# Moving the transposed activations by 16 bytes, and interleaving the stationary weights of two quarters of an up projection

## The chip, the cores and the metric

One core of one Trainium2 chip runs the whole program in one launch. The metric is device microseconds per execution; the time given for a kernel is the median of its runs.

## What is computed

The reference is one layer of a bidirectional encoder over 512 tokens of width 1024, in float32, with 256 memory tokens:

```python
x = x + token_mixer(rmsnorm(x, norm_mix), w_in, ...)      # HGRN2 heads and mLSTM heads, both directions
x = x + cross_attention(rmsnorm(x, norm_xattn), rmsnorm(mem, norm_mem), w_q, w_kv, w_o)
x = x + squared_relu_mlp(rmsnorm(x, norm_mlp), w_up, w_down)
return rmsnorm(x, norm_final)

def squared_relu_mlp(xn, w_up, w_down):                   # w_up: 1024 x 4096, w_down: 4096 x 1024
    return jnp.square(jax.nn.relu(xn @ w_up)) @ w_down
```

## The kernel before

**Three matmuls for one.** Every float32 operand of a projection is split into a high half, which has the type float32r, and the remainder as a low half. `mm3` (L221 to L223) multiplies high by high, high by low and low by high, and adds all three in PSUM. In the notation of the profile: L221 is stationary high and moving high, L222 stationary high and moving low, L223 stationary low and moving high.

**The weight stream.** All weights are packed by the host into 141 slices of 128 partitions by 1024 elements, in the order in which they are used (`SEQ`). `load` brings a slice into a buffer `st` by a DMA on SyncE's queue; `split` makes the halves `wh` and `wl` of it: an ACTIVATE on ScalarE (L217) writes the high half, a subtraction on VectorE (L218) the low half. There are three buffers each of `st`, `wh` and `wl`. `weights(key)` splits the slice that is needed and the two after it, and starts the load of the third after it.

**Two kinds of projection.** `proj_d` makes output with channels on partitions: the weights are stationary, 128x128 for each of eight k-tiles, and 512 tokens of activations move. A slice holds the eight k-tiles one behind the other, 128 columns (512 bytes in a partition) each: `z = slice(k * P, k * P + P)`. `proj_t` makes output with tokens on partitions: 128 tokens of activations are stationary, and 512 columns of weights move.

**Transposed activations.** The moving operand of a `proj_d` is a pair of tiles `xT` of 4096 elements, k-tiles 0 to 3 in the first, 4 to 7 in the second, each k-tile as 512 high and then 512 low elements. Three activations use the same pair in turn: the normed input (the mixer's projections), `x2T` (the query projection of the cross-attention) and `x3T` (the MLP's up projection). They are written piece by piece by L217 and L218, or by L769 and L770 in `transp`.

**The MLP.** It runs over four quarters f of the 4096 hidden channels. In each, eight slices of the up projection give eight `act` tiles (ReLU on ScalarE at L872, square on VectorE at L873, split by L217 and L218), and then `proj_t` multiplies these by eight slices of the down projection (residual add at L887). `act` lies in tiles of the tag `yT` in quarters 0 and 2, and in tiles of the tag `a4` (`a` in the profile) in quarters 1 and 3. A quarter's up and down projections have 192 matmuls of 512 columns each.

**Dependent work.** The chains of the mixer's heads advance by `tick()` between the projections. HGRN's `hgrn_chain` multiplies, level by level (L = 1, 2, 4, ... 64), a `rhs` that is gathered in place (L372), updates tiles with strided accesses (L422, L425, L429), and gathers a `kcomb` (L362):

```python
rhs=ap(q2, w * P, [2 * L, P // (2 * L)], [512 + L, 2], [1, L])     # L372
fa = ap(f, 0, [512, 2], [2 * L, nb])                               # L429, in place: fa = fa * fb
fb = ap(f, L, [512, 2], [2 * L, nb])
```

The mLSTM's chain takes two tiles of the tag `tiny2` for each of four token tiles of a head (`nd` and `rd`, L631 to L638).

**Where tiles lie.** A tag's buffers lie one behind the other, in the order in which the tags are first used, each rounded up to 32 bytes: ... `misc`, `selr`, `xT` (2 buffers of 16384 bytes), `st`, six tiny ones, `wh`, `wl` (3 of 4096 each), `a4` (10 of 4096), `t2`, `vv`, ... `yT` (8 of 4096), `tiny4`, `tiny2`. This gives the byte address in a partition: `xT` at 52512 and 68896, the first `wh` at 97760, the first `a4` at 122336, the first `yT` at 196160. [...]

The order of instructions on each engine is chosen by the tile framework's scheduler; `weights` asks for high priority.

Of the kernel before, what the change touches and what calls it, by code (L numbers as in the profile page):

```python
# [10 lines left out]
F32 = mybir.dt.float32  # L11
F32R = mybir.dt.float32r
# [6 lines left out]
P = 128  # L19
# [10 lines left out]

# columns of the per-channel vector pack
V_XATTN, V_MEM, V_MLP = 0, 8, 16
# [5 lines left out]

# columns of the constant pack
C_ID, C_MF, C_MB, C_SEL, NC1 = 0, 128, 256, 384, 392  # L40
# [35 lines left out]
def trunk(ctx: ExitStack, tc: tile.TileContext, x, mem, wpk, vec, cst, lmask, rmask, rows, out):  # L76
# [20 lines left out]
    def tiny(w):  # L97
        return sb.tile([P, w], F32, tag=f"tiny{w}", name=nm("tiny"), bufs=2 if w == 8 else 6)

    def ap(t, off, *dims):  # L100
        a = t[:, :]
        return bass.AP(a.tensor, a.offset + off, [list(a.ap[0])] + [list(d) for d in dims])
# [5 lines left out]
    VV = lambda: T("vv", 516, 8)  # L108
    XT = lambda: [T("xT", 4096, 2, F32R) for _ in range(2)]
    YT1 = lambda dt=F32R: T("yT", 1024, 8, dt)  # L110
    hl = lambda t: (t[:, 0:512], t[:, 512:1024])

# [1 line left out]
    cs = sb.tile([P, NC1], F32, name="cs")  # L114
# [50 lines left out]

# [1 line left out]
    chains = []  # L167
# [20 lines left out]

# [1 line left out]
    st_tiles, hl_tiles = {}, {}  # L190
# [8 lines left out]
    def split(i):  # L199
        if i >= len(SEQ) or i in hl_tiles:  # L200
            return
        load(i)
        s = st_tiles[i]
        hi, lo = T("wh", 1024, 3, F32R), T("wl", 1024, 3, F32R)
        split_out(hi, lo, s)
        hl_tiles[i] = (hi, lo)

    def weights(key):
# [15 lines left out]

    # activation operand accessors: list over k of (hi [P,n], lo [P,n])
    def xk(tiles, n=512):
# [7 lines left out]
    def proj_d(mat, c0, xs, n=512, count=2):  # L234
        """[128 channels, n tokens] PSUM tiles, one per slice"""
        for j in range(count):
            wh, wl = weights(("d", mat, 0, c0 + P * j))
            ps = mmb()
            for k in range(8):
                z = slice(k * P, k * P + P)  # L240
                mm3(ps[:, :n], wh[:, z], wl[:, z], xs[k][0], xs[k][1], k == 0, k == 7)
                if k == 3:
                    tick()
            yield ps
            tick()

    def proj_t(mat, k0, c0, xs, ntile=4, pre=None, late=False):
        """token-major [128 tokens, 512] PSUM tiles over 8 k-tiles (four slices)"""
        acc = [mmb() for _ in range(ntile)]

        def part(t, q, w):
            for k in range(2):
                kk = 2 * q + k
                xh, xl = xs[kk][0][:, t * P:t * P + P], xs[kk][1][:, t * P:t * P + P]
                z = slice(k * 512, k * 512 + 512)
                mm3(acc[t], xh, xl, w[0][:, z], w[1][:, z], kk == 0, kk == 7)

        for q in range(2 if late else 3):
            w = weights(("t", mat, k0 + 2 * q, c0))
            for t in range(ntile):  # L260
                part(t, q, w)
                if t % 2 == 1:
                    tick()
        if pre is not None:
            pre()
        tail = [(q, weights(("t", mat, k0 + 2 * q, c0))) for q in range(2 if late else 3, 4)]
        for t in range(ntile):
            for q, w in tail:
                part(t, q, w)
            yield t, acc[t]  # L270
            if t % 2 == 1:
                tick()

# [1 line left out]
    xT = XT()  # L275
# [25 lines left out]

# [1 line left out]
    vh = []  # L303
# [11 lines left out]

# [1 line left out]
    ys = [None] * 8  # L317
# [26 lines left out]
    def hgrn_chain(h, s_):  # L344
        q, f, k = s_["q"], s_["f"], s_["k"]
        q2 = A4()  # [b | f]
        v.tensor_tensor(out=q2[:, 0:512], in0=q[:, 0:512], in1=f[:, 512:1024], op=ALU.mult)
# [20 lines left out]
        for li, L in enumerate(LEVELS):  # L368
# [10 lines left out]
            yield  # L379
        # L = 128: adjacent windows  # L380
        ps = smb()
        for b in range(2):
            w0, w1 = slice(b * 256, b * 256 + P), slice(b * 256 + P, b * 256 + 256)
            pe.matmul(ps[:, b * 256 + P:b * 256 + 256], lhsT=k[:, w0], rhs=q2[:, 512 + b * 256 + P:512 + b * 256 + 256], start=True, stop=True)
            pe.matmul(ps[:, b * 256:b * 256 + P], lhsT=k[:, 512 + b * 256 + P:512 + b * 256 + 256], rhs=q2[:, w0], start=True, stop=True)
        # A[s-tile 2b, window 2b+1] and A[s-tile 2b+1, window 2b]
        sc.activation(ap(A, P, [1024 + 256, 2], [1, P]), ap(ps, P, [256, 2], [1, P]), AF.Copy)
        sc.activation(ap(A, 512, [1024 + 256, 2], [1, P]), ap(ps, 0, [256, 2], [1, P]), AF.Copy)
        update(q2, k, f, 128)
        yield  # L390
        # L = 256
        for dr in range(2):
# [38 lines left out]
    def head_out(o, gate, gcol, idx):  # L431
        """o [128 tokens, 4 x 128]: per-head norm, transpose, gain, gate, split into yT"""
        junk = T2()
# [17 lines left out]

# [1 line left out]
    ml = {}  # L453
# [11 lines left out]
    def gates_chain():  # L465
        grow = ml["grow"]
        ps = smb()
        for t in range(4):
            pe.transpose(ps[:, t * P:t * P + P], grow[:, t * P:t * P + P], ident)
        gt = sb.tile([P, 64], F32, name="gt")   # [w, (ig f, ig b, fg f, fg b), h]  # L470
        v.tensor_copy(gt[:, :].rearrange("p (w g h) -> p w g h", g=4, h=4), ap(ps, 0, [P, 4], [32, 4], [1, 4]))
# [17 lines left out]
        for _ in range(4):  # L489
            yield  # L490
        # token-major sums of the log forget gate
        tri = A4()
        nc.sync.dma_start(out=tri[:, 0:640], in_=cst[:, NC1:NC_])
        pb = smb()
        for i, c in enumerate((C_INC, C_SUF, C_ISUF, C_PRE, C_ONE)):
            pe.matmul(pb[:, i * 32:i * 32 + 32], lhsT=tri[:, c:c + P], rhs=lf, start=True, stop=True)
        bd = sb.tile([P, 128], F32, name="bd")  # [gap 0..3][w][dir,h]
        b4 = lambda g, w, dr: bd[:, g * 32 + w * 8 + dr * 4:g * 32 + w * 8 + dr * 4 + 4]
# [14 lines left out]
        yield  # L513
        # rows: forward heads on partitions 0..3, backward heads on 32..35
        lp = A4()
# [33 lines left out]
        for t in range(4):  # L549
            pe.transpose(ps[:, t * 64:t * 64 + 64], mr[0:64, t * P:t * P + P], ident[0:64, 0:64])  # L550
        em = sb.tile([P, 32], F32, name="em")  # [w, dir, h]
        sc.activation(em[:, :].rearrange("p (w g h) -> p w g h", g=2, h=4), ap(ps, 0, [64, 4], [32, 2], [1, 4]), AF.Exp, scale=-1.0)
# [89 lines left out]

# [1 line left out]
    hst = {}  # L644
# [52 lines left out]
    mo1 = gate_proj(4352, V_MO + 2, False)  # L697
    # memory tokens: norm and transposes
    mt = [A4(), A4()]
# [26 lines left out]

# [1 line left out]
    kT = [A4(F32R) for _ in range(4)]   # per head: [d-tile][hi 256 | lo 256]  # L728
    for i in range(4):
# [10 lines left out]

# [1 line left out]
    xr = {}  # L742
# [9 lines left out]
    def proj_res(mat, k0, src, tgt, st, pre=None):  # L752
        """residual add of a token-major projection; transposes of finished token tiles"""
        for c in range(2):
            for t, ps in proj_t(mat, k0, 512 * c, src, pre=pre if c == 0 else None):
                v.tensor_tensor(out=xr[t, c], in0=ps, in1=xr[t, c], op=ALU.add)
                stats(st, t, c)
                transp(tgt, t, c)
# [29 lines left out]

# [1 line left out]
    os_ = [None] * 8  # L790
# [61 lines left out]

# [1 line left out]
    pending = []  # L854
# [138 lines left out]
```

## Time and profile before

| | |
|---|---|
| time, median of 3 runs | 904.14 us (903.22 to 904.22) |
| span of the profiled execution | 902.4 us |
| TensorE busy (matmuls) | 884.6 us, 98% of the span |
| TensorE weight loads, beside the matmuls | 728.2 us, 81% |
| VectorE, ScalarE, GpSimd busy | 55%, 41%, 2% |
| HBM traffic | 93 GB/s over the span |

The span runs from the first to the last instruction of one profiled execution; the median of the runs lies 1.7 us above it. A matmul's row in the profile is longer than the time from one start to the next, because matmuls are pipelined: what counts below is the **pitch**, the time from one matmul's start to the next one's, which is the length of an unbroken stretch divided by its number of matmuls.

### The profile page before, as it was taken

To read this page: it belongs to the slowest core of one execution; us is meant where nothing else is said; L and a number is where in the kernel's file an instruction comes from. 1 tells how busy PE (TensorE), PEld (TensorE's weight loads), DVE (VectorE), ACT (ScalarE), POOL (GpSimd) and SP (SyncE) were. 2 spreads that over 40 slices of the span, in tenths; PEclk is the share of its full clock that TensorE was granted. 3 is DMA by queue.
4 is the path that set the end of the run, shared out by engine and by line. 5 is a ranking of instruction groups with operands and counts; after the bars stand their busy time and mean duration, and the time that the engine had idled before them with its cause. 6 is when DMAs were issued, how large, how long until landed. Compare 5 with 4: busy or idle time off the path is not lost.

```text
span 902.4 us, 11028 instructions
## 1 busy us (share of the span) xinstructions
PE 884.6 (98%) x4290; PEld 728.2 (81%) x4290; DVE 498.0 (55%) x863; ACT 371.8 (41%) x701; POOL 19.5 (2%) x49
## 2 busy tenths in 40 slices
PE   7999999999999999999999999999999999999996
PEld 5887888888876987887888888888888888888885
DVE  5457688689346977654455445433444344334443
ACT  5235443352358567454444445421332133113432
POOL 1000000010010000000000000000000000000001
PEclk9999999999999999999999999999999999999998
DMA  6321122221141232422111222222222222222212
GB/s 253 132 100 71 70 75 76 107 73 57 47 140 70 100 110 96 153 80 94 70 70 48 70 94 93 94 94 94 94 93 94 95 108 100 95 94 94 93 47 94
DMA packets 24614, 84.21 MB, mean 93 GB/s; under 512 B 2865, under 2 KB 2993, under 8 KB 24562
## 3 DMA queue, kind: packets, MB, share of 16 engines
q1 hardware_dynamic: 24272, 83.04, 25.2%
q8 instruction: 34, 0.56, 0.2%
q10 hardware_dynamic: 290, 0.47, 0.1%
q14 instruction: 18, 0.15, 0.0%
HBM read 81.40 MB, written 2.10 MB: 93 GB/s over the span
## 4 chain that ended last, share of the span: by engine, by line
PE 67%; DVE 1%; ACT 1%; issue 0%; POOL 0%; POOLq 0%; ACTq 0%
PE mm L223 20%; PE mm L222 20%; PE mm L221 20%; PE sm L625 2%; PE sm L610 2%; PE sm L764 1%; PE sm L222 1%; PE sm L221 1%; PE sm L223 1%; PE sm L821 0%; PE sm L595 0%; DVE wl L218 0%; DVE xT L770 0%; ACT wh L217 0%; POOL tiny L163 0%
## 5 line engine op out<-in xcount | busy, mean ns | idle before, releaser
L218 DVE TENSOR_TENSOR wl<-st,wh 128x1024 fp32r<-128x1024 f32 x141 | 172.7, 1224 | 272.9 <-ACT wh L217 269.5
L217 ACT ACTIVATE wh<-st 128x1024 fp32r<-128x1024 f32 x141 | 149.2, 1058 | 312.7 <-PE mm L223 167.7
L221 PE MATMUL mm<-xT,wh 128*128 128x512 f32 x552 | 221.0, 401 | 0.0
L223 PE MATMUL mm<-xT,wl 128*128 128x512 f32 x552 | 218.1, 395 | 0.0
L222 PE MATMUL mm<-xT,wh 128*128 128x512 f32 x552 | 217.6, 394 | 0.2 <-DVE xT L770 0.2
L223 PEld LDWEIGHTS mm<-xT,wl 128*128 128x128 f32 x552 | 104.1, 189 | 23.4 <-issue 0.6
L222 PEld LDWEIGHTS mm<-xT,wh 128*128 128x128 f32 x552 | 104.1, 189 | 22.6 <-DVE xT L770 0.8
L221 PEld LDWEIGHTS mm<-xT,wh 128*128 128x128 f32 x552 | 104.3, 189 | 22.4 <-issue 1.5
L223 PE MATMUL mm<-wh,yT 128*128 128x512 f32 x256 | 102.1, 399 | 0.0
L221 PE MATMUL mm<-wh,yT 128*128 128x512 f32 x256 | 102.0, 398 | 0.0
L222 PE MATMUL mm<-wl,yT 128*128 128x512 f32 x256 | 101.6, 397 | 0.0
L221 PE MATMUL mm<-wh,a 128*128 128x512 f32 x160 | 63.4, 396 | 0.0
L222 PE MATMUL mm<-wl,a 128*128 128x512 f32 x160 | 62.4, 390 | 0.0
L223 PE MATMUL mm<-wh,a 128*128 128x512 f32 x160 | 62.3, 390 | 0.0
L222 PEld LDWEIGHTS mm<-wl,yT 128*128 128x128 f32 x256 | 48.2, 188 | 11.3
L221 PEld LDWEIGHTS mm<-wh,yT 128*128 128x128 f32 x256 | 48.2, 188 | 11.3
L223 PEld LDWEIGHTS mm<-wh,yT 128*128 128x128 f32 x256 | 48.2, 188 | 11.3
L222 PEld LDWEIGHTS mm<-wl,a 128*128 128x128 f32 x160 | 30.1, 188 | 6.6 <-issue 0.5
L221 PEld LDWEIGHTS mm<-wh,a 128*128 128x128 f32 x160 | 30.0, 188 | 6.6 <-issue 0.5
L223 PEld LDWEIGHTS mm<-wh,a 128*128 128x128 f32 x160 | 30.0, 188 | 6.2
L372 PEld LDWEIGHTS sm<-a,t 128*128 128x128 f32 x224 | 30.1, 191 | 2.2 <-ACT t L362 0.4
L887 DVE SCALAR_TENSOR_TENSOR vv<-mm,misc,vv 128x512 f32<-128x512 f32 x32 | 23.3, 748 | 13.7 <-PE mm L223 13.5
(222 smaller groups left out, 1118.7 us busy)
## 6 DMA issues: line engine op xcount, KB each, us to landing
st<-in_wpk SPq DMA_DIRECT2D x141, 512.0 KB, 3.2
as<-in_x SPq DMA_DIRECT2D x4, 512.0 KB, 6.4
vv<-in_x SPq DMA_DIRECT2D x8, 256.0 KB, 4.1
out<-vv SPq DMA_DIRECT2D x7, 256.0 KB, 2.2
a<-in_mem SPq DMA_DIRECT2D x2, 512.0 KB, 3.6
t<-in_rows SPq DMA_DIRECT2D x2, 256.0 KB, 5.9
gate<-in_rows SPq DMA_DIRECT2D x1, 512.0 KB, 4.9
a<-in_lmask SPq DMA_DIRECT2D x1, 448.0 KB, 8.1
```

Source lines behind the costliest of these rows:

```text
L217: sc.activation(dst_hi, src, AF.Copy)
L218: v.tensor_tensor(out=dst_lo, in0=src, in1=dst_hi.bitcast(F32), op=ALU.subtract)
L221: pe.matmul(ps, lhsT=ah, rhs=bh, start=first, stop=False)
L222: pe.matmul(ps, lhsT=ah, rhs=bl, start=False, stop=False)
L223: pe.matmul(ps, lhsT=al, rhs=bh, start=False, stop=last)
L372: pe.matmul(ps[:, z], lhsT=kc[:, z], rhs=ap(q2, w * P, [2 * L, P // (2 * L)], [512 + L, 2], [1, L]), start=True, stop=True)
L610: pe.matmul(ps, lhsT=k[:, ws * P:ws * P + P], rhs=q, start=True, stop=True)
L625: pe.matmul(ps[:, dr * 129:dr * 129 + 129], lhsT=St[:, col:col + P], rhs=mv[ws][:, h * 129:h * 129 + 129], start=(i == 0), stop=(i == len( ...
L764: pe.transpose(ps[:, k * P:k * P + P], xr[t, c][:, k * P:k * P + P], ident)
L887: v.scalar_tensor_tensor(out=z, in0=ps, scalar=r2[:, t:t + 1], in1=z, op0=ALU.mult, op1=ALU.add)
```

## The change

Three things are changed; comments are dropped as well.

`XT` allocates tiles of 4104 elements and hands out elements 4 to 4099 of them, so every access to a transposed activation lies 16 bytes further on in its tile. The pair of tiles is 64 bytes longer than before, so the first `xT` is used from 52528 and the second from 68944, and all tags allocated later move up by 64 bytes. The tag `tiny2` has five buffers in place of six, 32 bytes less.

`lanes(key)` is 1 for every slice except those of the up projection's quarters 2 and 3, for which it is 2 and 8. `split` writes the halves of such a slice so that in each group of 2 (or 8) k-tiles column c of every k-tile comes before column c + 1 of any: the k-tile's columns lie 8 (or 32) bytes apart. The DMA of the slice and `st` are as before; the ACTIVATE and the subtraction write, and the subtraction reads the high half, with that step. `proj_d` loads the stationary operand with a step of g elements. The moving operand, the number of instructions and the sums computed stay the same.

```diff
     def tiny(w):
-        return sb.tile([P, w], F32, tag=f"tiny{w}", name=nm("tiny"), bufs=2 if w == 8 else 6)
+        return sb.tile([P, w], F32, tag=f"tiny{w}", name=nm("tiny"), bufs=2 if w == 8 else (5 if w == 2 else 6))
 
     def ap(t, off, *dims):
-        a = t[:, :]
+        a = t if isinstance(t, bass.AP) else t[:, :]
         return bass.AP(a.tensor, a.offset + off, [list(a.ap[0])] + [list(d) for d in dims])
...
-    XT = lambda: [T("xT", 4096, 2, F32R) for _ in range(2)]
+    XT = lambda: [T("xT", 4104, 2, F32R)[:, 4:4100] for _ in range(2)]
...
         hi, lo = T("wh", 1024, 3, F32R), T("wl", 1024, 3, F32R)
-        split_out(hi, lo, s)
+        n = lanes(SEQ[i])
+        if n == 1:
+            split_out(hi, lo, s)
+        else:
+            dims = ([1024 // (8 // n), 8 // n], [1, n], [n, P])
+            split_out(ap(hi, 0, *dims), ap(lo, 0, *dims), s[:, :].rearrange("p (a b c) -> p a b c", b=n, c=P))
         hl_tiles[i] = (hi, lo)
+
+    def lanes(key):
+
+        if key[1] != "up" or key[3] < 2048:
+            return 1
+        return 2 if key[3] < 3072 else 8
...
             ps = mmb()
+            g = lanes(("d", mat, 0, c0 + P * j))
             for k in range(8):
-                z = slice(k * P, k * P + P)
-                mm3(ps[:, :n], wh[:, z], wl[:, z], xs[k][0], xs[k][1], k == 0, k == 7)
+                z = (k // g * g * P + k % g, [g, P])
+                mm3(ps[:, :n], ap(wh, *z), ap(wl, *z), xs[k][0], xs[k][1], k == 0, k == 7)
```

## The prediction, made before the change was run

> **What bounds the kernel now.** I read the page first: busy shares, the slices over time and the chain that ended last.
>
> ```profile
> span 902.4 us, 11028 instructions
> ...
> PE 884.6 (98%) x4290; PEld 728.2 (81%) x4290; DVE 498.0 (55%) x863; ACT 371.8 (41%) x701; POOL 19.5 (2%) x49
> ...
> PE   7999999999999999999999999999999999999996
> ...
> PEclk9999999999999999999999999999999999999998
> ...
> PE 67%; DVE 1%; ACT 1%; issue 0%; POOL 0%; POOLq 0%; ACTq 0%
> PE mm L223 20%; PE mm L222 20%; PE mm L221 20%; PE sm L625 2%; PE sm L610 2%; PE sm L764 1%; PE sm L222 1%; PE sm L221 1%; PE sm L223 1%; PE sm L821 0%; PE sm L595 0%; DVE wl L218 0%; DVE xT L770 0%; ACT wh L217 0%; POOL tiny L163 0%
> ```
>
> TensorE has work in every slice, at full clock, and the chain is its three matmul lines. So the time is the number of matmuls times their pitch, and what the change does to the pitch is what it does to the time. A busy TensorE is no TensorE at its peak, so I took the MLP's eight stages one by one (windows: length, busy time and count per engine).
>
> ```profile
> core 0: us, PE busy (x) PEld busy (x) DVE busy (x) ACT busy (x) POOL busy (x), PEclk, DMA share, GB/s
> 541.16:585.66 44.50, 44.50 (x198) 36.38 (x196) 23.25 (x38) 20.22 (x36) 0.00 (x0) 1.00 0.27 95
> 585.66:630.63 44.97, 44.97 (x194) 36.16 (x192) 16.00 (x17) 9.60 (x10) 0.00 (x0) 1.00 0.25 94
> 630.63:674.58 43.95, 43.95 (x193) 36.06 (x192) 19.62 (x23) 16.31 (x22) 0.00 (x0) 1.00 0.26 96
> 674.58:718.15 43.57, 43.57 (x193) 36.03 (x192) 15.99 (x17) 9.60 (x10) 0.00 (x0) 1.00 0.27 97
> 718.15:762.12 43.97, 43.97 (x194) 36.06 (x192) 19.63 (x23) 16.30 (x22) 0.00 (x0) 1.00 0.26 96
> 762.12:807.10 44.98, 44.98 (x194) 36.16 (x193) 16.00 (x17) 9.60 (x10) 0.00 (x0) 1.00 0.26 94
> 807.10:851.04 43.94, 43.94 (x193) 36.06 (x192) 19.63 (x23) 16.29 (x22) 0.00 (x0) 1.00 0.26 96
> 851.04:894.75 43.71, 43.71 (x193) 35.85 (x191) 18.21 (x27) 13.49 (x24) 2.21 (x3) 1.00 0.13 49
> ```
>
> Up and down alternate; each has 192 matmuls and no gap. The pitch of up is 43.95 / 192 = 228.9 ns. Down with `yT` stationary (585.66, 762.12) has 44.97 / 192 = 234.2 ns, down with `a4` stationary (674.58) 43.57 / 192 = 226.9 ns. The two downs differ in nothing but where the stationary tile lies, under the same load of the other engines: 7.3 ns of pitch hang on the placement of the two operands. This is the resource that both edits touch.
>
> What would the pitch be without that? Plain float32 matmuls of 512 columns (L610), and the short ones of the HGRN levels (L372), on the timeline:
>
> ```profile
> 97.93 1.48 PE L372 MATMUL sm<-a,t 128*128 128x128 f32 x8
> ...
> 106.07 1.12 PE L372 MATMUL sm<-a,t 128*128 128x128 f32 x8
> ...
> 120.80 1.05 PE L372 MATMUL sm<-a,t 128*128 128x128 f32 x8
> ...
> 281.98 1.02 PE L610 MATMUL sm<-yT 128*128 128x512 f32 x2
> ...
> L610 PE MATMUL sm<-yT x32: 590/592/688, 282.0 to 350.1; 128*128 128x512 f32 x32
> ```
>
> Two L610 take 1.02 us with the last one's 0.59 us, so their pitch is 0.43 us for 512 columns, 0.84 ns a column. The up projection's float32r matmuls stream about twice as fast; at just twice, 512 columns would take 215 ns, which I take as the floor (an estimate). Up then loses 14 ns a matmul, `a4` 12, `yT` 19. The last row of L372 (level 8, runs of eight) gives (1.05 - 0.28) / 7 = 110 ns for 128 columns with a weight load of 128 columns beside: a load streams in 110 ns or less, and is hidden under 229 ns.
>
> So the loss is not the load's length. My reading is that the load and the moving operand meet in memory: the load walks 128 x 4 bytes at 0.86 ns a column, the moving operand 4 bytes in 0.42 ns, twice as fast, so it overtakes the load's position and the two collide, the more or less often according to where they begin.
>
> **The change part by part.** *16 bytes further on.* The row below counts the matmuls that move `xT`: 3 x 552 = 1656, of which 384 are in the two re-laid quarters.
>
> ```profile
> L221 PE MATMUL mm<-xT,wh 128*128 128x512 f32 x552 | 221.0, 401 | 0.0
> L218 DVE TENSOR_TENSOR wl<-st,wh 128x1024 fp32r<-128x1024 f32 x141 | 172.7, 1224 | 272.9 <-ACT wh L217 269.5
> L217 ACT ACTIVATE wh<-st 128x1024 fp32r<-128x1024 f32 x141 | 149.2, 1058 | 312.7 <-PE mm L223 167.7 <-PE mm L222 110.0 <-issue 31.7
> ```
>
> Stationary minus moving address, modulo 256 bytes (the period is an assumption; three pairs cannot prove it): `a4` to `wh` 0 with 226.9 ns, `wh` to `xT` 192 with 228.9, `yT` to `wh` 96 with 234.2. After: 240 for the first `xT` (52528 against 97824), 208 for the second, the others unchanged because all later tags move alike. 240 is nearest to the full period (226.9), 208 to today's 192 (228.9); half and half gives 227.9, so I take -1.0 ns on 1272 matmuls, **-1.3 us**. The ends are the best and the worst pair seen: -2.0 ns (-2.5 us) and +5.3 ns (+6.7 us). Below that nothing but the floor: -14 ns, -17.8 us.
>
> *Two k-tiles column by column (quarter 2).* Columns are 8 bytes apart, so the load now walks 8 bytes in 0.86 ns: exactly the moving operand's pace. Two walks at the same pace either never meet or meet all the time, and the one that has to wait once falls behind and is then out of the way. I expect the loss to go nearly: 14 ns x 192 = **-2.7 us**. [...] The nearest row for two elements from a place is the second L372 row (level 2): (1.12 - 0.28) / 7 = 120 against 110 ns, +10 ns, +1.9 us.
>
> *Eight k-tiles (quarter 3).* [...] The nearest row is the first of L372 (level 1, each next element from another place, though for the moving operand): (1.48 - 0.33) / 7 = 164 ns, 54 ns more than level 8. A load so slowed would take 164 ns and still be under 229, so its length is covered; if the 54 ns add to the pitch, it is +10.4 us. The lower end is the floor, -2.7 us. The meetings are more but short; I take +2.5 ns, **+0.5 us**, nearer to the covered case because 229 ns leave 65 to spare.
>
> *The splits.* ScalarE and VectorE write, and VectorE reads, with the step. What a step costs them is in these rows (L429 works on elements 8, 16 and 32 bytes apart as its size falls; L613 has whole runs):
>
> ```profile
> L422 DVE TENSOR_TENSOR a<-a,a 128x512 f32<-128x512 f32 x28 | 19.3, 689 | 2.7 <-PE sm L372 2.6
> ...
> L429 DVE TENSOR_TENSOR a<-a 128x512 f32<-128x512 f32 x4 | 2.7, 674 | 0.0
> L429 DVE TENSOR_TENSOR a<-a 128x256 f32<-128x256 f32 x4 | 2.4, 609 | 0.0
> L613 DVE TENSOR_TENSOR as<-as,sm 128x256 f32<-128x256 f32 x4 | 1.7, 416 | 0.0
> L429 DVE TENSOR_TENSOR a<-a 128x128 f32<-128x128 f32 x4 | 1.6, 410 | 0.0
> L613 DVE TENSOR_TENSOR as<-as,sm 128x128 f32<-128x128 f32 x4 | 1.1, 284 | 0.0
> ...
> 723.63 1.06 ACT L217 ACTIVATE wh<-st 128x1024 fp32r<-128x1024 f32 x1 [4.22 <-PE mm L222]
> 724.60 0.58 ACT L872 ACTIVATE t<-mm 128x512 f32<-128x512 f32 x1
> ...
> 729.18 1.06 ACT L217 ACTIVATE wh<-st 128x1024 fp32r<-128x1024 f32 x1 [1.96 <-PE mm L222]
> ```
>
> At 8 bytes nothing (674 against 689 ns), at 32 bytes (410 - 284) / 128 = 1.0 ns an element. Quarter 3's subtraction goes from 1.22 to about 2.2 us, the ACTIVATE to at most about as much from 1.06. A slice comes every 5.5 us (723.63 to 729.18); VectorE's share of it rises from 2.5 (19.63 / 8) to 3.5 us and ScalarE's from 2.0 to 3.2. A split begins when its `wh` buffer is given free, two slices (11 us) ahead of its use, and takes 4.4 us at most. Cost nothing; without that cover it would be 8 x 2.1 = 17 us. Behind them on VectorE wait the squares and splits of `act`, which the down projection needs only microseconds later.
>
> *The rest.* Five `tiny2` for six: a head's token tile takes two, so a buffer comes back two and a half tiles later, long after its readers; nothing. SyncE's loads are untouched, the count of instructions too.
>
> Sum: -1.3 - 2.7 + 0.5 = -3.5 us. Against the profiled execution, 902.4 - 3.5 = 898.9 us of span; the median of the runs stands 1.7 us above that span, so **900.6 us** from 904.1.
>
> [...] The trace has VectorE at full pace with two elements in 16 bytes and at about 0.7 of it with one (416 against 609 ns, fixed parts included). [...]
>
> **The rivals.** *The eight-lane load stalls the stream* (the other side). Place: 192 matmuls of quarter 3; price up to 54 ns; it decides the sign from 21 ns a matmul on, where it eats the other 4.0 us. For it: L372's level 1, L429 at 32 bytes. Against: the load has slack. Full price: 904.1 - 4.0 + 10.4 = 910.5 us; half of it 905.3.
>
> *The new offset is a bad one.* All `xT` matmuls go to the 234.2 ns of the `yT` pair: +6.7 us with -2.7 + 0.5, 908.6 us. For it: one of the three pairs is that bad. Against: 240 and 208 lie by the two good ones.
>
> *Nothing happens.* The pitch is set by something else than the meeting of the two reads, or gains and losses cancel: 904 us.
>
> *The odd 16 bytes end the collisions everywhere.* No pair seen has an odd multiple of 16 between its tiles. At the floor on all 1656: 904.1 - 23.2 = 880.9 us; half of it 892.5.
>
> **How the numbers follow.** Forecast (897 to 902) 0.42; eight lanes dear 0.23; bad offset 0.10; nothing 0.17; collisions end 0.08. The forecast's own range is 897 to 902.5. Faster by over 0.2% (1.8 us, about what a measurement tells from no change) is the first and last, 0.50; same 0.17; slower 0.33. The range 893 to 911 leaves out most of the last case and the dearest end of eight lanes.
>
> **What would show it.** [...] L218 and L217 longer in quarter 3 alone, with no idle TensorE before its slices. The prediction is wrong if quarter 2 does not fall, or if the downs move, for then it is not the meeting of the walks.

## The result, and the profile after

The changed kernel takes 908.88 us (median, 908.63 to 910.22); the kernel before took 903.68 us on the same chip (902.71 to 904.22). The ratio is 1.0061, 95% interval 1.0047 to 1.0075: slower by 5.2 us, where 3.5 us of gain had been forecast. The profiled execution has a span of 907.2 us against 902.4.

First the page of the changed kernel: span, busy times, and the chain of work that ended last.

```profile
span 907.2 us, 11028 instructions
...
PE 889.6 (98%) x4290; PEld 740.7 (82%) x4290; DVE 506.3 (56%) x863; ACT 381.7 (42%) x701; POOL 19.6 (2%) x49
...
PE 68%; DVE 1%; ACT 1%; issue 0%; POOL 0%; POOLq 0%; ACTq 0%
```

The same number of instructions, and still TensorE from one end to the other. Its busy time grew by 5.0 us, the loads' by 12.5. So the pitch has to be read stage by stage. The windows of the changed kernel's eight MLP stages, up and down in turn (length, then busy time and count per engine, clock, DMA share, GB/s):

```profile
core 0: us, PE busy (x) PEld busy (x) DVE busy (x) ACT busy (x) POOL busy (x), PEclk, DMA share, GB/s
541.14:586.00 44.86, 44.86 (x198) 36.39 (x196) 23.24 (x38) 20.22 (x36) 0.00 (x0) 1.00 0.26 94
586.00:630.97 44.97, 44.97 (x193) 36.16 (x192) 16.00 (x17) 9.61 (x10) 0.00 (x0) 1.00 0.27 94
630.97:675.29 44.32, 44.32 (x193) 36.07 (x192) 19.62 (x23) 16.31 (x22) 0.00 (x0) 1.00 0.26 95
675.29:718.84 43.55, 43.55 (x193) 36.04 (x192) 15.99 (x17) 9.73 (x10) 0.00 (x0) 1.00 0.27 97
718.84:763.52 44.68, 44.68 (x193) 37.49 (x192) 19.62 (x23) 16.67 (x22) 0.00 (x0) 1.00 0.26 94
763.52:808.53 45.01, 45.01 (x194) 36.01 (x192) 16.99 (x16) 12.10 (x10) 0.00 (x0) 1.00 0.23 83
808.53:855.72 47.19, 47.19 (x193) 47.15 (x193) 26.89 (x25) 22.98 (x22) 0.00 (x0) 1.00 0.28 100
855.72:899.50 43.78, 43.73 (x193) 35.86 (x191) 18.23 (x28) 13.51 (x24) 2.26 (x3) 1.00 0.14 49
```

Set beside the windows of before: quarters 0 and 1 grew by 0.36 and 0.37 us, quarter 2 by 0.71, quarter 3 by 3.25; the downs stayed. That is 4.7 us of the 4.8 us between the spans. In pitch (44.32, 44.68 and 47.19 us over 192): 230.8 ns with the offset alone, 232.7 with two lanes, 245.8 with eight, where all had 228.9. ("Lanes" are the k-tiles that are held column by column in turn: a load's columns lie 4, 8, 16 or 32 bytes apart with 1, 2, 4 or 8 lanes.)

In quarter 3 the column of the weight loads (PEld) says something new: 47.15 us of 47.19, where the other stages have 36 to 37.5. The lines of the changed kernel have other numbers than before: the matmuls L221 to L223 are now L232 to L234, the splits L217 and L218 are L228 and L229. The groups below are kept apart by shape: the load of one line in quarter 1 of the kernel before (first row), then the changed kernel in quarter 2 (three rows) and quarter 3 (three rows); count, busy us, mean ns, then idle time before:

```profile
L222 PEld LDWEIGHTS mm<-xT,wh 128*128 128x128 f32 x63 | 11.8, 188 | 2.6
...
L233 PEld LDWEIGHTS mm<-xT,wh 128*128 128x128 f32 x64 | 12.5, 195 | 2.4
L229 DVE TENSOR_TENSOR wl<-st,wh 128x1024 fp32r<-128x1024 f32 x8 | 9.8, 1227 | 18.7 <-ACT wh L228 18.7
L228 ACT ACTIVATE wh<-st 128x1024 fp32r<-128x1024 f32 x8 | 8.9, 1114 | 20.2 <-PE mm L233 15.9 <-PE mm L234 4.3
...
L233 PEld LDWEIGHTS mm<-xT,wh 128*128 128x128 f32 x64 | 21.1, 330 | 0.0
L229 DVE TENSOR_TENSOR wl<-st,wh 128x1024 fp32r<-128x1024 f32 x8 | 16.1, 2010 | 13.8 <-ACT wh L228 13.8
L228 ACT ACTIVATE wh<-st 128x1024 fp32r<-128x1024 f32 x8 | 15.4, 1930 | 9.8 <-PE mm L233 6.2 <-PE mm L234 3.3
```

The load's row goes from 188 ns (one lane) to 195 and 330, and at 330 it has no idle time left: a row is now longer than the pitch, so each load begins before the row of the one ahead has ended. The splits cost VectorE and ScalarE more in quarter 3, but they wait, and TensorE does not.

### The profile page after: what moved, and what is told of

Same layout as the page of the kernel before. It is cut to its first block, busy times and chain, and to the rows that moved or that the text cites. A ratio compares the mean times of both kernels' runs of the same rounds, so it can differ in the third digit from the quotient of the medians.

```text
span 907.2 us, 11028 instructions
## 1 busy us (share of the span) xinstructions
PE 889.6 (98%) x4290; PEld 740.7 (82%) x4290; DVE 506.3 (56%) x863; ACT 381.7 (42%) x701; POOL 19.6 (2%) x49
## 4 chain that ended last, share of the span: by engine, by line
PE 68%; DVE 1%; ACT 1%; issue 0%; POOL 0%; POOLq 0%; ACTq 0%
PE mm L233 20%; PE mm L234 20%; PE mm L232 20%; PE sm L637 2%; PE sm L622 2%; PE sm L776 1%; PE sm L233 1%; PE sm L232 1%; PE sm L234 1%; PE sm L833 0%; PE sm L607 0%; DVE wl L229 0%; DVE xT L782 0%; ACT wh L228 0%; POOL tiny L163 0%
## 5 line engine op out<-in xcount | busy, mean ns | idle before, releaser
L229 DVE TENSOR_TENSOR wl<-st,wh 128x1024 fp32r<-128x1024 f32 x141 | 181.3, 1286 | 270.1 <-ACT wh L228 266.4
L228 ACT ACTIVATE wh<-st 128x1024 fp32r<-128x1024 f32 x141 | 159.4, 1130 | 301.9 <-PE mm L234 165.1
L232 PE MATMUL mm<-xT,wh 128*128 128x512 f32 x552 | 222.7, 405 | 0.0
L234 PE MATMUL mm<-xT,wl 128*128 128x512 f32 x552 | 219.2, 397 | 0.0
L234 PEld LDWEIGHTS mm<-xT,wl 128*128 128x128 f32 x552 | 113.4, 205 | 21.1 <-issue 0.6
L232 PEld LDWEIGHTS mm<-xT,wh 128*128 128x128 f32 x552 | 113.5, 206 | 20.5 <-issue 1.7
L233 PEld LDWEIGHTS mm<-xT,wh 128*128 128x128 f32 x552 | 113.5, 206 | 19.9 <-DVE xT L782 0.8
L234 PE MATMUL mm<-wh,yT 128*128 128x512 f32 x256 | 102.1, 399 | 0.0
L232 PE MATMUL mm<-wh,yT 128*128 128x512 f32 x256 | 101.9, 398 | 0.0
L232 PE MATMUL mm<-wh,a 128*128 128x512 f32 x160 | 63.4, 396 | 0.0
L234 PE MATMUL mm<-wh,a 128*128 128x512 f32 x160 | 62.3, 390 | 0.0
L232 PEld LDWEIGHTS mm<-wh,yT 128*128 128x128 f32 x256 | 48.2, 188 | 11.3
L234 PEld LDWEIGHTS mm<-wh,yT 128*128 128x128 f32 x256 | 48.2, 188 | 11.3
L232 PEld LDWEIGHTS mm<-wh,a 128*128 128x128 f32 x160 | 30.1, 188 | 6.6 <-issue 0.5
L234 PEld LDWEIGHTS mm<-wh,a 128*128 128x128 f32 x160 | 30.0, 188 | 6.2
L384 PE MATMUL sm<-a,t 128*128 128x128 f32 x224 | 30.9, 285 | 0.0
```

Of the source, the lines that this page charges most:

```text
L228: sc.activation(dst_hi, src, AF.Copy)
L229: v.tensor_tensor(out=dst_lo, in0=src, in1=dst_hi.bitcast(F32), op=ALU.subtract)
L232: pe.matmul(ps, lhsT=ah, rhs=bh, start=first, stop=False)
L233: pe.matmul(ps, lhsT=ah, rhs=bl, start=False, stop=False)
L234: pe.matmul(ps, lhsT=al, rhs=bh, start=False, stop=last)
L384: pe.matmul(ps[:, z], lhsT=kc[:, z], rhs=ap(q2, w * P, [2 * L, P // (2 * L)], [512 + L, 2], [1, L]), start=True, stop=True)
```

## The experiments

Pitches below are taken from the starts of the matmuls in the trace, slice by slice (24 matmuls each); a window's length over 192 is up to 1 ns more, and 3 ns more in quarter 0, where a few matmuls of the first slice start late.

**1 and 2: each part alone.** One kernel keeps the new offset and holds every slice in one lane; the other keeps the old places (and six `tiny2`) and has the lanes.

```diff
 # shift_only, against the changed kernel
-        if key[1] != "up" or key[3] < 2048:
-            return 1
-        return 2 if key[3] < 3072 else 8
+        return (1, 1, 1, 1)[key[3] // 1024] if key[1] == "up" else 1
 # lanes_only, against the changed kernel
-    XT = lambda: [T("xT", 4104, 2, F32R)[:, 4:4100] for _ in range(2)]
+    XT = lambda: [T("xT", 4096, 2, F32R) for _ in range(2)]
```

> Only the 16-byte offset of the transposed activations (and five tiny2 buffers), all weight halves laid out as before. In the changed kernel quarter 1 of the up projection, which has the offset and no interleaving, went from 228.9 to 230.8 ns a matmul. Theory A (the offset costs about 1.9 ns wherever an xT tile moves, and nothing else): quarters 1, 2 and 3 of the up projection each 230.8 ns (44.1 us in place of 43.7), the downs unchanged at 234.2 and 226.9 ns, the whole 1 to 3 us slower than before, 905 to 907 us. Theory B (the offset is neutral as a whole and all of the loss is in the interleaved quarters): 904 us within 0.7 us.

> Only the interleaving (quarter 2 with two k-tiles, quarter 3 with eight), xT tiles where they were. Theory L (in quarter 3 the weight load, with each element 32 bytes from the last, streams for longer than the moving operand and sets the pitch): quarter 3 keeps about 246 ns, load rows stay near 331 ns, whatever the offset; quarter 2 loses what the offset cost, 230 to 231 ns. Theory C (in quarter 3 the load and the moving operand collide more often; the pitch is a matter of where they meet): with the tiles placed otherwise quarter 3 moves by 5 ns or more from 246. Theory M (the prediction's: a load at the moving operand's pace, quarter 2, can keep clear of it, but the 16 bytes put them on top of each other): quarter 2 falls to 215 to 222 ns here. By L the whole is 3 to 4 us slower than before, 907 to 908 us; by M 904 to 905.

The offset alone: 906.56 us against 903.15, ratio 1.0035 (1.0021 to 1.0049). All four ups have the pitch that the changed kernel's first two have (windows of the four ups of this kernel):

```profile
540.80:585.67 44.87, 44.87 (x197) 36.41 (x196) 23.22 (x38) 20.21 (x36) 0.00 (x0) 1.00 0.27 94
630.64:674.96 44.32, 44.32 (x193) 36.07 (x192) 19.61 (x23) 16.30 (x22) 0.00 (x0) 1.00 0.27 95
718.51:762.86 44.35, 44.35 (x194) 36.08 (x192) 19.61 (x23) 16.30 (x22) 0.00 (x0) 1.00 0.27 95
807.83:852.15 44.32, 44.32 (x193) 36.07 (x192) 19.61 (x23) 16.29 (x22) 0.00 (x0) 1.00 0.27 95
```

The lanes alone: 907.81 us, ratio 1.0049 (1.0036 to 1.0061); quarters 0 and 1 stay at 228.9 ns. Windows of this kernel's quarters 2 and 3:

```profile
716.72:761.57 44.85, 44.85 (x194) 37.49 (x193) 19.61 (x23) 16.70 (x23) 0.00 (x0) 1.00 0.26 94
806.59:853.82 47.23, 47.23 (x194) 47.18 (x194) 27.27 (x25) 23.06 (x23) 0.00 (x0) 1.00 0.29 100
```

Two lanes give 233.3 ns, eight 245.0. So theory L holds for quarter 3 (the old places change nothing there), but not for quarter 2, where it put 230 to 231 ns; and quarter 2 did not fall to 215 to 222, as theory M had it. Each part makes the kernel slower by itself. They do not add: the offset costs where there is one lane, and in the two quarters with lanes it makes no odds (44.85 and 47.23 us at the old places, 44.68 and 47.19 at the new).

**3 and 4: is the load the bound?** Lanes 1, 2, 4, 8 in the four quarters at the old places; then the same with the up projection's matmuls cut to 256 tokens, so that each load stands beside half the matmul, and there are twice as many of both.

```diff
 # lanes_1248
+        return (1, 2, 4, 8)[key[3] // 1024] if key[1] == "up" else 1
 # half_1248, besides
+            m = n // 2 if mat == "up" else n
+            for c in range(0, n, m):
+                for k in range(8):
...
+                    mm3(ps[:, c:c + m], ap(wh, *z), ap(wl, *z), xs[k][0][:, c:c + m], xs[k][1][:, c:c + m], k == 0, k == 7)
...
```

> No offset; quarters 0, 1, 2, 3 of the up projection with 1, 2, 4 and 8 k-tiles interleaved (elements of a load 4, 8, 16, 32 bytes apart). Theory L: load rows of 188, 195, about 250 to 331 and 331 ns; the pitch stays near 229 to 231 ns as long as the row is under about 310 ns (row less 80 ns is the streaming time), and is the row less 85 ns above that: quarters 0 to 3 at 229, 230, 229 to 246, 246 ns. [...] Output as the reference's.

> As the kernel with 1, 2, 4 and 8 k-tiles by quarter, but the up projection moves 256 tokens at a time, so each of its matmuls is half as long and there are twice as many loads (384 a quarter). The moving operand then needs about 107 ns a matmul, and a load that streams longer shows as the pitch. Theory L: quarter 3's pitch stays near 246 ns (each matmul waits for its load), quarter 2's (16 bytes) somewhere from 170 to 246, quarters 0 and 1 about 117 to 125 ns. Theory C (collisions add to the moving time): quarter 3 at 107 plus 14 plus about 17, 135 to 145 ns, quarter 2 the same. The whole is slower by 4 x 192 short matmuls, 30 to 60 us.

With full matmuls (one run, 908.69 us) 228.9, 233.3, 240.0 and 245.0 ns. Halved (one run, 1001.98 us), the windows of quarters 0 to 3, now with 384 matmuls each:

```profile
541.30:587.02 45.72, 45.72 (x389) 45.67 (x388) 23.24 (x38) 20.20 (x36) 0.00 (x0) 1.00 0.27 93
632.00:678.08 46.08, 46.08 (x385) 46.08 (x384) 19.61 (x23) 16.81 (x22) 0.00 (x0) 1.00 0.25 92
721.66:811.14 89.48, 89.48 (x385) 89.48 (x385) 25.10 (x25) 22.00 (x22) 0.00 (x0) 1.00 0.15 53
856.20:948.76 92.56, 92.56 (x385) 92.56 (x385) 26.34 (x25) 22.56 (x22) 0.00 (x0) 1.00 0.15 52
```

This decides it for quarter 3. Half the columns to stream, and quarters 2 and 3 still take 233 and 241 ns for each pair (89.48 and 92.56 us over 384), while one and two lanes drop to 119 and 120. So with half the matmul beside it a load of 128 columns takes 233 and 241 ns when its columns are 16 or 32 bytes apart, 1.8 and 1.9 ns a column, against at most 0.93 and 0.94 (119 and 120 over 128) at 4 and 8 bytes. That is longer than the 228.9 ns in which a matmul of 512 tokens follows the other with one lane; with 512 tokens the pitch is 240.0 and 245.0 ns, and the load sets it.

**5: a map of places.** The weight halves get tiles of 1088 elements, and each slice starts in them at an offset of its own: in the ups 0 to 240 bytes by 16, with one lane (quarters 0, 1) and two (2, 3); in the downs 32, 64, 96 or 160.

```diff
+        o = place(SEQ[i])
+        hi, lo = (T(w, 1088, 3, F32R)[:, o:o + 1024] for w in ("wh", "wl"))
...
```

> No offset of xT. The wh and wl tiles are 256 bytes longer (one st buffer fewer pays for it; all tiles keep their address modulo 256), and each up-projection slice writes its halves at another offset: quarters 0 and 1, as laid out before, at 0, 16, ... 240 bytes; quarters 2 and 3, two k-tiles interleaved, at the same sixteen offsets. The downs move their halves by 32 and 64 bytes (quarters 0 and 1) and 96 and 160 (quarters 2 and 3). Theory R (the pitch follows stationary minus moving address modulo 256): quarter 1 of offsets, 64 bytes (difference 0) 227 ns; 0 bytes (192) 229; 160 bytes (96) 234; down with yT at 96 bytes (difference 0) 227 in place of 234, at 160 bytes (192) 229; down with a4 at 160 bytes (96) 234 in place of 227. Theory X (it is yT's or the weights' own place in memory, not the difference): downs keep 234 and 227 ns whatever the offset. For two k-tiles, the prediction's step says that some offsets give 215 to 222 ns; if all sixteen lie at 227 to 238, a load at the moving operand's pace gains nothing anywhere. Output as the reference's.

One run, 907.86 us. The windows of the two halves of the second down (`a4`, weights 32 and then 64 bytes on) and of the third (`yT`, 96 and then 160), 96 matmuls each:

```profile
675.96:698.35 22.39, 22.39 (x98) 17.99 (x96) 8.27 (x9) 5.35 (x6) 0.00 (x0) 1.00 0.26 94
698.35:720.32 21.97, 21.97 (x97) 18.04 (x96) 7.73 (x8) 4.37 (x4) 0.00 (x0) 1.00 0.28 96
764.95:786.76 21.81, 21.81 (x97) 18.02 (x96) 8.27 (x9) 5.36 (x6) 0.00 (x0) 1.00 0.27 97
786.76:808.76 22.00, 22.00 (x98) 18.04 (x97) 7.72 (x8) 4.37 (x4) 0.00 (x0) 1.00 0.27 96
```

With the weights 96 bytes on, `yT` is at difference 0 and falls from 234.2 to 226.7 ns, the pitch that `a4` had; with the weights 64 on, `a4` is at 192 and has 228.9, as `xT` had; in the last down, with the weights 160 on, `a4` is at 96 and has 234.2, as `yT` had. In these three cases one number, the difference of the two start addresses modulo 256, carries over from tile to tile. It is no smooth curve: `a4` with the weights 32 on is at 224, between the two good differences 192 and 0, and takes 233.2 ns (22.39 / 96). For the ups, two lanes gave between 230 and 234 ns at all sixteen offsets: nowhere the gain that the prediction had counted on. (In the ups the offset changes from slice to slice, and with one lane some slices do not have the pitch of their own difference: the slices at 240 and 16, on either side of the one at 0, read 227.5 and 227.0 ns, where a whole stage takes 228.3 and 233.3. Runs 11 and 12 hold a whole stage, or half of one, at one offset for that reason.)

**6 and 10: which walk makes the loss?** Some operands read less, so these two kernels do not compute the up projection. In the first, by quarter: nothing changed; the load reads one element 128 times; the moving operand reads one element 512 times; both. In the second the moving operand reads 256 elements twice each in a row, 128 four times each, 256 in two passes, 128 in four passes.

```diff
 # still
...
+                z = (k * P, [0 if f in (1, 3) else 1, P])
...
+                if f in (2, 3):
+                    xh, xl = ap(xh, 0, [0, n]), ap(xl, 0, [0, n])
 # slow_read, for the up projection alone
...
+                    d = (([1, 256], [0, 2]), ([1, 128], [0, 4]), ([0, 2], [1, 256]), ([0, 4], [1, 128]))[c0 // 1024]
+                    xh, xl = ap(xh, 0, *d), ap(xl, 0, *d)
```

> No offset, nothing interleaved. Quarter 0 of the up projection as before; in quarter 1 the loads read one element 128 times (step 0), in quarter 2 the moving operand is one element 512 times, in quarter 3 both. So quarters 1 to 3 do not compute the up projection. Theory M (the 14 ns above 215 are the two reads meeting in memory): quarters 1 and 2 fall to 215 to 219 ns, quarter 3 too. Theory F (they are a fixed price of a float32r matmul and its load): all four stay at 227 to 231 ns.

> Nothing moved or interleaved. The up projection's moving operand reads fewer elements of memory: in quarter 0 each of 256 elements twice in a row, in quarter 1 each of 128 four times in a row, in quarter 2 the same 256 elements in two passes, in quarter 3 128 elements in four passes. So the up projection is not the reference's. Theory B (the 14 ns come from the moving operand's rate of reading: it needs nearly all of what the memory gives, and the load's 128 reads push it back): quarters 0 and 1, at half and a quarter of the rate, fall to 215 to 219 ns, quarters 2 and 3, at the full rate, stay at 226 to 235. Theory S (a start-up price of each moving read, or of changing weights): all four stay at 226 to 235.

One run each, 898.63 and 897.91 us. Windows of quarters 0 to 3 of the first, then of quarters 0 to 2 of the second (quarter 3 has 43.95 us):

```profile
540.07:584.57 44.50, 44.50 (x198) 36.38 (x197) 23.25 (x38) 20.20 (x36) 0.00 (x0) 1.00 0.27 95
629.54:674.02 44.48, 44.48 (x193) 36.26 (x192) 19.61 (x23) 16.30 (x22) 0.00 (x0) 1.00 0.27 95
717.56:759.00 41.44, 41.44 (x193) 36.29 (x192) 19.61 (x23) 16.26 (x22) 0.00 (x0) 1.00 0.28 102
803.98:845.42 41.44, 41.44 (x194) 36.29 (x193) 19.61 (x23) 16.25 (x22) 0.00 (x0) 1.00 0.28 102
```

```profile
539.74:581.76 42.02, 42.02 (x197) 36.60 (x196) 23.23 (x38) 20.19 (x36) 0.00 (x0) 1.00 0.29 101
626.74:668.18 41.44, 41.44 (x193) 36.29 (x192) 19.61 (x23) 16.27 (x22) 0.00 (x0) 1.00 0.28 102
711.72:755.68 43.96, 43.96 (x193) 36.06 (x192) 19.62 (x23) 16.30 (x22) 0.00 (x0) 1.00 0.27 96
```

A load that does not walk at all costs the matmuls 231.7 ns (44.48 us), more than one that walks (228.9). So the loss does not come from one walk overtaking the other. Where the moving operand repeats each element, even only twice (quarter 0 of the second; from its second slice on), the pitch is 215.8 (41.44 us), whether the load walks or not; where it takes a new element every time, it is 228.9, though it covers but half or a quarter of the addresses. In these runs the loss exists only while the moving operand reads a new element at every step.

**8: the direction.** The moving operand of the ups runs backwards (and the ReLU reads PSUM backwards, so that the sums land where they did); offsets of 0 to 240 bytes by 32 or from 16, lanes 1, 2, 2, 1.

```diff
...
+                    xh, xl = ap(xh, n - 1, [-1, n]), ap(xl, n - 1, [-1, n])
...
```

> No offset of xT, weight halves at another offset in each slice of the up projection (quarters 0 and 1: 0, 32, ... 224 bytes; quarters 2 and 3: 16, 48, ... 240), quarters 1 and 2 with two k-tiles interleaved, 0 and 3 with one. In all four the moving operand is read from its last token to its first (step -1), and the ReLU reads the PSUM tile backwards. Theory W (a weight load reads its columns from the last to the first, so that in the changed kernel it ran against the moving operand and met it however they were placed; the prediction had the pace right and the direction wrong): with both falling at the same pace, quarters 1 and 2 drop to 215 to 222 ns at most offsets, while quarters 0 and 3 (half the pace) stay at 225 to 238. Theory N (no walks: neither direction nor pace counts, only that there are 128 reads): all four at 227 to 235 ns, as in the map of places. Output as the reference's.

One run, 907.94 us: 233.3 ns at nearly every offset with one lane and with two (236.5 at a few). If two walks at one pace had ever been in or out of step, turning one round would have mattered by lane count. It did not; that idea was given up here. No offset gave the 226.7 ns that difference 0 has otherwise, so the map of run 5 is shown only for operands that are both read forwards.

**7 and 9: all tiles at one place.** The page of before suggests a better version as soon as the map is known: the buffers of `st`, `wh`, `wl`, `a4` and `yT`, all of them multiples of 256 bytes, are allocated right behind `xT`, so that every pair has the difference 0. The rest is the kernel before. Then the same with `xT` used from 16 bytes on (and a wider `xT`, two `st`).

```diff
 # aligned
     xT = XT()
+    for tag, n, b in (("st", 1024, 3), ("wh", 1024, 3), ("wl", 1024, 3), ("a4", 1024, 10), ("yT", 1024, 8)):
+        T(tag, n, b)
 # aligned_16, besides (st with 2 buffers)
+    XT = lambda: [T("xT", 4160, 2, F32R)[:, 4:4100] for _ in range(2)]
```

> The kernel before, with only the order of allocation changed: st, wh, wl, a4 and yT right behind xT, so that xT, wh, wl, a4 and yT all start at the same address modulo 256 bytes (difference 0 for every projection). Theory R (pitch follows the difference modulo 256): up 226.7 ns in place of 228.9, down with yT 226.7 in place of 234.2, so the MLP's eight stages about 43.5 us each; over the 1656 matmuls that move xT, 768 with yT and 192 with xT stationary, 3.6 + 5.8 + 1.3 = 10.7 us less, 893 to 896 us. If the period is not 256 bytes or the place itself counts, some of the stages keep 44 to 45 us.

> The kernel with xT, wh, wl, a4 and yT at one address modulo 256, and then the 16 bytes of the change: xT tiles of 4160 elements, used from element 4, so that both halves begin 16 bytes above the others modulo 256 (difference 240 for both; in the changed kernel they had 240 and 208). One st buffer fewer pays for the 512 bytes. Theory R with the map of places (differences 240, 0 and 16 all gave 226.7 ns for a slice of its own): up keeps 226.7 ns, the whole 894 to 896 us, so the 16 bytes by themselves cost nothing and the change lost by the two halves' unequal and partly bad differences. Rival (an odd 16 bytes cost by themselves): up at 230 to 232 ns, the whole 900 to 903 us.

All at one place: **894.48 us** against 903.02, ratio 0.990 (0.9883 to 0.9916). It beats both kernels. 16 bytes off: 901.51 against 904.05, ratio 0.998 (0.9971 to 0.9989). Windows of the first: down with `yT`, up, down with `a4`; then of the second: down, up.

```profile
580.43:623.96 43.53, 43.53 (x194) 36.04 (x193) 15.99 (x17) 9.61 (x10) 0.00 (x0) 1.00 0.28 97
623.96:667.47 43.51, 43.51 (x193) 36.03 (x192) 19.61 (x23) 16.30 (x22) 0.00 (x0) 1.00 0.27 97
667.47:710.99 43.52, 43.52 (x193) 36.04 (x192) 15.99 (x17) 9.61 (x10) 0.00 (x0) 1.00 0.28 97
```

```profile
583.92:627.49 43.57, 43.57 (x193) 36.04 (x192) 15.99 (x17) 9.60 (x10) 0.00 (x0) 1.00 0.28 97
627.49:671.97 44.48, 44.48 (x194) 36.10 (x192) 19.61 (x23) 16.30 (x22) 0.00 (x0) 1.00 0.28 95
```

226.6 to 226.7 ns in every stage, and 231.7 in the ups as soon as `xT` starts 16 bytes further on. The second expectation had taken the slices at 240 and 16 of run 5 at their word and put 226.7; its rival, that an odd 16 bytes cost by themselves, gave the time.

**11: whose 16 bytes?** Aligned, then the weights alone are moved, one offset for a whole stage or half a stage. In the ups the weights are the stationary operand, in the downs the moving one, so that the same difference can be made by moving either. `place` gives the offset (bytes over 4; by quarter in the ups, by down projection and half in the downs); `wh` and `wl` are 1088 wide as in run 5.

```diff
+        if key[1] == "up":
+            return [[16, 16, 16, 16, 16, 16, 16, 16], [32, 32, 32, 32, 32, 32, 32, 32], [240, 240, 240, 240, 240, 240, 240, 240], [128, 128, 128, 128, 128, 128, 128, 128]][key[3] // 1024][key[3] % 1024 // P] // 4
+        if key[1] == "down":
+            return {(0, 0): 16, (0, 1): 240, (1, 0): 32, (1, 1): 224, (2, 0): 48, (2, 1): 128, (3, 0): 16, (3, 1): 240}[key[2] // 8, key[3] // 512] // 4
```

> All projection tiles at one address modulo 256, xT without offset; the weight halves (256 bytes longer, one st buffer fewer) begin some bytes further on, the same for a whole stage: up quarters 0 to 3 at 16, 32, 240, 128 bytes, where the weights are stationary; downs, where they move, quarter 0 at 16 then 240, quarter 1 at 32 then 224, quarter 2 at 48 then 128, quarter 3 at 16 then 240 (first and second half of the stage). Theory O (a moving operand that begins at an odd multiple of 16 bytes costs by itself, a stationary one doesn't): up quarters 0 and 2 stay at 226.7 ns, the downs at 16, 240 and 48 bytes are at 231 to 233, with 32, 224 and 128 as the difference says (228 to 235). Theory D (only the difference counts, and neighbouring slices carried the good pitch over in the map of places): up quarter 2 (difference 240) at 231.7 as in the last run, and the downs with the same difference (16 bytes on: 240) at 231.7 too, whoever moves. Output as the reference's.

One run, 905.95 us. The windows: down (`yT`) with the weights 16 bytes on, difference 240; the same 240 bytes on, difference 16; the quarter 2 up with the weights 240 on, difference 240; the first half of the third down with the weights 48 on, difference 208.

```profile
583.71:605.95 22.24, 22.24 (x97) 18.05 (x96) 8.27 (x9) 5.37 (x6) 0.00 (x0) 1.00 0.28 95
605.95:628.64 22.69, 22.69 (x98) 18.27 (x97) 7.72 (x8) 4.25 (x4) 0.00 (x0) 1.00 0.26 93
...
718.23:762.07 43.84, 43.84 (x194) 36.02 (x193) 19.62 (x23) 16.31 (x22) 0.00 (x0) 1.00 0.27 96
762.07:784.46 22.39, 22.39 (x97) 18.13 (x96) 8.27 (x9) 5.36 (x6) 0.00 (x0) 1.00 0.27 95
```

Difference 240 costs 228.3 ns (43.84 / 192) if the stationary operand was moved and 231.7 (22.24 / 96) if the moving one was; difference 16 costs 233.3 and 236.4. So at these two differences there are two terms: the difference, and about 3 ns for a moving operand that begins at an odd multiple of 16 bytes. Neither expectation had both. A difference of 32 bytes gives 233.3 whichever was moved. The two terms are not the whole rule: at difference 208, with the moving operand 48 bytes on, the last row gives 233.2 ns (22.39 / 96), while the k-tiles 4 to 7 of run 1, which move the second `xT` at the same difference, take 229.9 to 230.5.

**12: the lanes at the best place.** `aligned` with lanes 1, 2, 4, 8.

```diff
+        return (1, 2, 4, 8)[key[3] // 1024] if key[1] == "up" else 1
```

> All projection tiles at one address modulo 256, no offset; quarters 0 to 3 of the up projection with 1, 2, 4, 8 k-tiles interleaved. If the load's streaming time sets the pitch of quarter 3, it stays at 240 to 246 ns with load rows near 331 although the place is the best one; quarter 2 (309 ns rows before) at 233 to 240. Quarter 1 (two k-tiles): by the prediction's walk at one pace 215 to 220 ns; by what the runs showed since (the load's 128 reads take turns with a moving operand that has no slack, wherever they are) 226 to 234, no better than quarter 0's 226.7.

One run, 900.78 us. The windows of quarters 1 to 3:

```profile
623.63:668.43 44.80, 44.80 (x194) 37.05 (x193) 19.61 (x23) 16.69 (x22) 0.00 (x0) 1.00 0.27 94
711.96:757.07 45.11, 45.11 (x193) 45.08 (x193) 25.18 (x25) 22.11 (x22) 0.00 (x0) 1.00 0.31 104
800.61:847.61 47.00, 47.00 (x194) 46.95 (x194) 26.69 (x25) 23.10 (x23) 0.00 (x0) 1.00 0.29 101
```

Two lanes are 6.6 ns a matmul dearer than one even here (233.3 against 226.7), and with four and eight (235.0 and 244.8) the loads fill the stage: 45.08 of 45.11 us and 46.95 of 47.00. That the load's reads take turns with the moving operand's, as the expectation puts it, fits these numbers, but no run isolates it.

## Why the prediction was wrong

*What bounds the kernel, and the floor: right.* The time is the number of matmuls times their pitch, before and after. The floor of 215 ns, an estimate from plain float32 matmuls, is there: 215.8 in runs 6 and 10, where the moving operand repeats its elements. But no placement tried reaches it; the best is 226.6.

*The reading behind all sizes: wrong.* "The load and the moving operand meet in memory" was inferred from two downs that differ in placement alone. That difference is real. What was made of it, a walk that overtakes the other and meets it less at equal pace, is refuted: a load that does not walk costs more than one that does (231.7 against 228.9), and a load at the moving operand's pace gains nothing at any of sixteen offsets (230 to 234), nor at difference 0 (233.3 against 226.7), nor with the other operand turned round (233.3). That the two reads hinder each other in some other way is not refuted; the pitch does follow the difference of their addresses.

*16 bytes further on: -1.0 ns was taken, +1.9 came.* The assumed period of 256 bytes holds for the three differences that run 5 gives to other pairs of tiles (0, 96 and 192). What failed is the pitch that was read off for the new differences. In quarter 1 of run 1 the k-tiles 0 to 3, which move the first `xT` (240), take 231.8 ns, where 226.9 was put, and the k-tiles 4 to 7 (208) take 229.9, where 228.9 was put. Two things stand behind that. The three known differences were joined as if nothing lay between them, but 224 takes 233.2 (run 5); that 240 with an aligned moving operand comes to 228.3 (run 11), near the value put, is luck. And the change moves the moving operand to an odd multiple of 16 bytes, which none of the three pairs of before has, and at difference 240 that alone costs about 3 ns (run 11). The prediction named the absence, but only in a rival that took it for a gain.

Sum for quarters 0 and 1: +0.73 us. Over the 888 earlier matmuls that move `xT` the mean time from one of them to the next (starts under 400 ns apart) went from 234.4 to 236.3 ns, +1.9 as in the MLP, some 1.7 us. In these two profiles it does not show in the time at which the MLP begins (541.16 and 541.14), because longer gaps among them differ as well: 15 with 6.9 us before, 7 with 3.5 after. The offset alone cost 3.4 us in the medians, of which 1.5 are the four ups and about 1.7 these.

*Two k-tiles: -2.7 us was taken, +0.71 came.* This is the step that made the forecast a gain, and it rests on the meeting walks alone. The nearest row, +10 ns from short matmuls, was too dear; the stage's own price is +3.7 ns (with the offset; +4.4 without, run 2). The loads still had slack (2.4 us of idle time before the 64 of one line), so their length is not what costs.

*Eight k-tiles: +0.5 us was taken, +3.25 came.* The step "a load so slowed would take 164 ns and still be under 229, so its length is covered" failed. The 164 ns came from a row where the *moving* operand had one element in each place; a *load* of 128 such columns takes 241 ns (run 4), and its cover of 229 ns is gone. Its cost is then the excess, 17 ns x 192. The rival "the eight-lane load stalls the stream" had the place, but its price of 54 ns was an addition to the pitch, where the runs show the longer of two lengths and a few ns more (241 ns for the load beside half the matmul, 245.8 beside the whole), and its threshold of 21 ns counted on gains elsewhere that did not come. No run shows the +2.5 ns a matmul that the sum has for this quarter; its pitch rose by 17 ns (228.9 to 245.8). The load's row is 188 and 195 ns at 4 and 8 bytes from column to column, and 312 and 331 at 16 and 32 (quarter 1 of the kernel before, quarters 2 and 3 of the changed one, and run 3 for 16 bytes), and the two short ones are hidden, the two long ones not; yet two lanes, with a row 7 ns longer than one lane's, cost 4 ns in pitch as well.

*The splits: right.* 2.01 and 1.93 us where about 2.2 and at most as much were put, and 1.11 us for ScalarE with two lanes; all of it is under the matmuls. *`tiny2` and the downs: right*, the downs at 44.97, 43.55 and 45.01 us. "The prediction is wrong if quarter 2 does not fall" was the test that caught it. The rival of the bad offset had put 908.6 us, and 908.9 came; that is luck, for it took 6.7 us for the offset, where run 1 measured 3.4, and a gain for the lanes, which cost 4.7 us by themselves (run 2).

*What stays open.* Why a moving operand at full rate loses 11 ns at the best difference (226.6 against 215.8) and up to 21 at the worst (236.4), why an odd 16 bytes cost it about 3 more at two differences, and why two lanes cost 4 to 7, was measured and not explained; also the slices of run 5 that seem to take their pitch from a neighbour, the two pitches at difference 208, and why no offset tried gives 226.7 ns when the moving operand runs backwards. No run has a moving operand at full rate without a load beside it, so how much of the 11 ns the load causes is not known.

## What to carry to other kernels

When TensorE is the bound and has no gaps, read the pitch of each stage as its length over its count: stages with equal work and unequal pitch (234.2 and 226.9 ns here) pointed to the placement of their operands, and giving all of them the same start modulo 256 bytes was worth 1.0% here, more than either edit of this change moved. A weight load was hidden here where its whole length, by its own access pattern, was under the matmul beside it (at most 119 ns at a step of 4 bytes, under a pitch of 228.9) and set the pitch where it was not (241 ns at 32 bytes, pitch 245.8), and a step of 8 bytes, hidden with at most 120 ns, cost 4 to 7 ns a matmul even so: look for a row of the same kind of instruction before pricing a stride, and read zero idle time before the loads (0.0 us in quarter 3, 2.4 in quarter 2) as the sign that the cover is gone. And if a gain rests on a mechanism that nothing in the trace isolates, give it the weight of a guess.

## What the runs showed of the hardware

- A float32r matmul of 512 columns with a load beside it, both operands read forwards and the moving one beginning at a multiple of 32 bytes, starts every 226.6 ns when the two start addresses are equal modulo 256, and by stationary minus moving address every 228.3 at 240, 228.9 at 192, 233.2 at 224, 233.3 at 16 and 32, 234.2 at 96; 215.8 when the moving operand repeats each element.
- A moving operand that begins at an odd multiple of 16 bytes costs about 3 ns a matmul more at differences 240 and 16 (231.7 against 228.3, 236.4 against 233.3).
- A weight load of 128 float32r columns: 188, 195, 312 and 331 ns in its row for columns 4, 8, 16 and 32 bytes apart; with half the matmul beside it, one came every 119, 120, 233 and 241 ns (the first two are upper bounds of its own length).
- Writing 1024 elements with a step of 32 bytes took ScalarE 1.93 us against 1.06, and VectorE (which also reads with it) 2.01 against 1.22.
